# A new head for a one-core encoder step: first weights in five pieces among the input tiles, squares behind the parts, a split sum for the total, four plain pairs

## Chip, cores and metric

The kernel runs on one core of one Trainium2 chip. The metric is the device time of one execution in microseconds. Three runs of the kernel before gave a median of 1302.38 us (1302.33 to 1303.26).

## What is computed

One layer of a streaming encoder for 512 new frames and 64 frames of a running stream, together T = 576 columns with D = 1024 features, in f32:

```python
x = x + 0.5 * swiglu_ffn(rms_norm(x, ffn1_norm), ffn1_w_gate_up, ffn1_w_down)
h = rms_norm(x, mix_norm); p = h @ w_in
# two convolution branches and a gated merge through w_a_out, w_b_out, w_out
x = x + merged @ w_out
x = x + 0.5 * swiglu_ffn(rms_norm(x, ffn2_norm), ffn2_w_gate_up, ffn2_w_down)
y = rms_norm(x, final_norm)

def swiglu_ffn(x, w_gate_up, w_down):
    gate, up = jnp.split(x @ w_gate_up, 2, axis=-1)
    return (jax.nn.silu(gate) * up) @ w_down
```

The change concerns the head: the first norm and the first columns of the first FFN (DFF = 2816, in 22 columns of 128).

## The kernel before

**Layout and products.** Features lie on the 128 partitions, the 576 columns on the free axis; x is eight tiles `X[0..7]`. A product of f32 accuracy is made of f32r products: every weight and every activation is split into a high part (a cast on ACT) and a low part (value minus high part). One step k of one output tile (`mm`, lines 392 to 403) is six matmuls of 128 x 288: high·high, high·low and low·high, for both halves of the columns. A full tile over eight k has 48 matmuls.

**Norm.** The gain is put into the operands (`split_scaled`, line 484); the inverse root R is multiplied in after the product. `Sum` (line 492) adds the eight squares. `total` multiplies the sum by a matrix of ones: with `gather` called before (line 527) the sum has been split into two f32r operands, otherwise it runs in plain f32, which PE does in two passes per matmul. `rstd` (line 549) takes the root on ACT and refines it by three DVE instructions.

**Gate and up columns.** Columns i < `PLAIN[f]` are plain: a gate tile g_i and an up tile u_i, 96 matmuls. The others are pairs by a scheme with seven half products (`pair`, 84 matmuls) that needs derived operands of x: `Forms.scale` (two ACT instructions), `combine` (four DVE instructions and two casts), `split` (two low parts), each for four indices p; and sums of weights on DVE. Before, the first three columns are plain.

**Order.** Each engine runs its instructions in the order in which the program writes them (`Ordered`, line 68). Weights come through `Stream` (line 193): `load` issues raw tiles on SP's queue into six slots, `begin` casts the high part on ACT and, for units marked "dma", writes the negative, to which a DMA of POOL adds the raw value; `end` makes the low part on DVE for the others. `get` keeps the stream six units ahead, so a product also issues casts and low parts of later weights.

**PSUM** is one pool of four tiles (`mmps`, line 126), two banks each. A tile's slot is free when its last reader in program order is done: for the total that is the tensor_scalar of `rstd`, for a gate tile the multiplication by R in `gate` (line 707), for an up tile that in `hidden` (line 711).

**The head** (lines 605 to 674): FIRST are the tiles g0, u0 and g1, multiplied together step by step as k arrives. Their weights come as nine raw tiles (k = 1, 3 and 4 steps at a time, `FIRST_KS`), alternating with the x tiles on SP's queue; the gains are ACT's first transfer. POOL makes three of the squares and the last three low parts. Then four units are prepared (u1 and g2), `scale(0)`, `scale(1)` and `combine(0)` follow, the eight steps of FIRST are multiplied with the total (plain f32) before the last, and u1 is multiplied. Inside `ffn`, the columns are then gated in turn, with steps of `Forms` given in a list and put between (`forming`); `split(0)` and `split(1)` make their low parts by POOL's DMA.

Of the kernel before, what the change touches and what calls it, by code (L numbers as in the profile page):

```python
# [20 lines left out]
KU = KT // 2  # L21
# [10 lines left out]
R_CA = 4  # L32
# [11 lines left out]

HALVES = ((0, H), (H, T))
LATE_SPANS = (((0, 304),), ((304, T),))
FIRST_KS = (1, 3, 4)
WARM = 10


PLAIN = {"f1": 3, "f2": 1}

IN_TURN = (0, 4, 1, 5, 2, 6, 3, 7)

# [1 line left out]
SIX = ((0, 0), (1, 0), (0, 1), (1, 1), (2, 0), (2, 1))  # L56
# [47 lines left out]
def tile_encoder_step(  # L104
# [44 lines left out]
    def psum2():  # L149
        return mmps.tile([P, 2, 512], F32, tag="mm", name=nm("mm"))  # L150
# [16 lines left out]
    ones = cpool.tile([P, P], F32, tag="ones", name="ones")  # L167
# [3 lines left out]
    pool.memset(eps, EPS)  # L171
    prm_src = params.rearrange("p (r j) -> p r j", j=KT)
    gains = cpool.tile([P, R_CA, KT], F32, tag="gains", name="gains")
    sca.dma_start(gains, prm_src[:, :R_CA, :])
    prm = cpool.tile([P, NPAR - R_CA, KT], F32, tag="prm", name="prm")
    hst = cpool.tile([P, KT, NHIST], F32, tag="hst", name="hst")
    X = [cpool.tile([P, T], F32, tag=f"x{j}", name=f"x{j}") for j in range(KT)]
    def table(func):

        t = cpool.tile([P, 1], F32, tag="table", name=nm("table"))  # L180
        sca.activation(t, eps, func)

    sca.copy(ones_r, ones)

    warm = psum2()
    for _ in range(WARM):
# [6 lines left out]
    class Stream:  # L193
# [108 lines left out]
    ws = Stream(6)  # L302
    plan = {}
    homes = [0]

    def home(other):

        homes[0] += 1
        return ("u", other)[homes[0] % 2]

    def plan_tile(name, w, row0, ks, col0, other, home_of=None):
        plan[name] = []
        for k in ks:
            r = ws.raw(w, row0, k, col0)
            plan[name].append(ws.unit(r, k, home_of or home(other), "dma"))
            row0 += k * P

    FIRST = [("f1", "g", 0), ("f1", "u", 0), ("f1", "g", 1)]

    def gu_col(part, i):  # L320
        return i * P + (DFF if part == "u" else 0)
# [22 lines left out]
    def plan_ffn(f, gu, dn):  # L344
        for g, grp in enumerate(GROUPS):
            for i in grp:
                if i >= PLAIN[f]:
                    plan_pair(f, gu, i)
                    continue
                for part in "gu":  # L350
                    if (f, part, i) not in plan:
                        plan_tile((f, part, i), gu, 0, (KU, KU), gu_col(part, i), "g")
            n = len(grp)
            for j in range(KT):
                late = f == "f2" and grp[-1] == FT - 1 and j in LATE
                plan_tile(
                    (f, "d", g, j), dn, grp[0] * P, (n - n // 2, n // 2), j * P, "g",
                    "act" if late else None,
                )

    for name in FIRST:
        plan[name] = []
    row = 0
    for k in FIRST_KS:
        for name in FIRST:
            r = ws.raw(ffn1_gu, row, k, gu_col(*name[1:]))
            plan[name].append(ws.unit(r, k, "act", "dve"))
        row += k * P
    plan_ffn("f1", ffn1_gu, ffn1_dn)

    def plan_mixer(name, w, col):
# [17 lines left out]
    plan_ffn("f2", ffn2_gu, ffn2_dn)  # L389


    def mm(ps, w, kk, xs, first, last, spans=HALVES):


        (whi, wlo), (xh, xl) = w, xs
        parts = ((whi, xh), (whi, xl), (wlo, xh))
        for n, s in SIX:
            if s < len(spans):
                (a, b), (i, e) = parts[n], spans[s]
                pe.matmul(  # L400
                    ps[:, s, : e - i], a[:, kk, :], b[:, i:e],
                    start=first and n == 0, stop=last and n == 2,
                )
# [64 lines left out]
    def low(v, hi):  # L468
        lo = atile(F32R)
        dve.tensor_tensor(lo, v, hi.bitcast(F32), op=ALU.subtract)  # L470
        return lo

    def low_by_dma(v, hi):
        lo = atile(F32R)
        sca.mul(lo, hi.bitcast(F32), -1.0)
        pool.dma_start(lo.bitcast(F32), v, accum_op=ALU.add)
        return lo

    def split(v):

        hi = high(v)
        return hi, low(v, hi)
# [66 lines left out]
    def rstd(total, spans=HALVES):  # L549

        a, t = ttile(), ttile()
        r = rpool.tile([P, T], F32, tag="r", name=nm("r"), bufs=2)
        tot = total.total(spans)
        span = slice(spans[0][0], spans[-1][1])
        shaped = halves if len(spans) == 2 else (lambda v: v)
        a, t, y = a[:, span], t[:, span], r[:, span]
        dve.tensor_scalar(shaped(a), tot, 1.0 / D, EPS, op0=ALU.mult, op1=ALU.add)
        sca.activation(y, a, AF.Abs_reciprocal_sqrt)
        dve.scalar_tensor_tensor(t, y, -0.5, y, op0=ALU.mult, op1=ALU.mult)
        dve.tensor_tensor(t, t, a, op=ALU.mult)  # L560
        dve.scalar_tensor_tensor(y, t, 1.5, y, op0=ALU.add, op1=ALU.mult)
        return r


    class Forms:
# [19 lines left out]
                dve.tensor_tensor(out, a, b, op=op)  # L585
            self.t[p] = [(v, high(v)) for v in (c, d)]

        def split(self, p, by_dma=False):
            self.parts[p] = [
                (hi, (low_by_dma if by_dma else low)(v, hi)) for v, hi in self.t.pop(p)  # L590
            ]

        def operands(self, xg):

# [10 lines left out]
    ss = Sum()  # L605
    xg = []
    def load(j):
        nc.sync.dma_start(X[j], x[j * P : (j + 1) * P, :])

    def begin(j):  # L610
        xg.append(split_scaled(X[j], par(j, R_N1)))

    def weights(lo=dve):
        for _ in FIRST:
            ws.prep(lo)

    def squares(*js):
        for j in js:
            ss.square(X[j], pool if j in (0, 2, 4) else sca)

    load(0)
    begin(0)
    squares(0)
    weights()
    load(1)
    begin(1)
    weights()
    load(2)
    load(3)
    begin(2)  # L630
    begin(3)
    squares(1, 2)
    weights(pool)
    for j in range(4, KT):
        load(j)
    ss.add(dve)
    ss.add(dve)
    squares(3)
    begin(4)
    begin(5)  # L640
    ss.add(dve)
    squares(5, 4)
    ss.add(dve)
    ss.add(dve)
    begin(6)
    begin(7)
    squares(6, 7)
    ss.add(dve)
    ws.eager = True
    for _ in range(4):  # L650
        ws.prep()
    forms1 = Forms(R_N1)
    forms1.scale(0)
    forms1.scale(1)
    forms1.combine(0)
    nc.sync.dma_start(prm, prm_src[:, R_CA:, :])
    table(AF.Abs_reciprocal_sqrt)
    first = {name: psum2() for name in FIRST}
    firstw = {}
    for name in FIRST:  # L660
        firstw[name] = []
        for n in plan[name]:
            w = ws.ready.pop(n)
            firstw[name] += [(w, kk) for kk in range(ws.units[n][1])]
    for k in range(KT):
        if k == KT - 1:
            R1 = rstd(ss)
        for name in FIRST:
            w, kk = firstw[name][k]
            mm(first[name], w, kk, xg[k], k == 0, k == KT - 1)  # L670
    early.update(first)
    name = ("f1", "u", 1)
    ps = product(name, xg)
    early[name] = ps


    def split_early(p):
        one.split(p, by_dma=True)

    def update(j, ps, R=None):  # L680

# [137 lines left out]
    ffn(  # L819
        "f1", xg, ss, finish1, one, R1,  # L820
        (
            ((split_early, 0), (one.scale, 2), (one.combine, 1)),
            ((split_early, 1), (one.scale, 3), (one.combine, 2)),
            ((one.split, 2), (one.combine, 3)),
            ((one.split, 3),),
        ),
# [370 lines left out]
```

## Time and profile before

| | |
|---|---|
| Median of three runs | 1302.38 us |
| The profiled execution | 1303.07 us, its span 1301.3 us |
| PE busy (matmuls) | 1286.3 us, 9746 instructions |
| DVE, ACT, POOL busy | 892.0, 778.5, 400.5 us |
| HBM read | 113.81 MB |

The span is what the profile shows from the first to the last instruction of the core. Busy times of PE contain the modelled tail of pipelined matmuls, so back-to-back matmuls are better told from their start times. A bracket behind a line of the timeline tells how long the engine was idle before it and what ended that.

### The profile page before, as it was taken

To read this page: it belongs to the slowest core of one execution; us is meant where nothing else is said; L and a number is where in the kernel's file an instruction comes from. 1 tells how busy PE (TensorE), PEld (TensorE's weight loads), DVE (VectorE), ACT (ScalarE), POOL (GpSimd) and SP (SyncE) were. 2 spreads that over 40 slices of the span, in tenths; PEclk is the share of its full clock that TensorE was granted. 3 is DMA by queue.
4 is the path that set the end of the run, shared out by engine and by line. 5 is a ranking of instruction groups with operands and counts; after the bars stand their busy time and mean duration, and the time that the engine had idled before them with its cause. 6 is when DMAs were issued, how large, how long until landed. Compare 5 with 4: busy or idle time off the path is not lost.

```text
span 1301.3 us, 25714 instructions
## 1 busy us (share of the span) xinstructions
PE 1286.3 (99%) x9746; PEld 1282.5 (99%) x9746; DVE 892.0 (69%) x1460; ACT 778.5 (60%) x1374; POOL 400.5 (31%) x502
## 2 busy tenths in 40 slices
PE   9999999999999999999999999999999999999997
PEld 8999999999999999999999999999999999999996
DVE  6758758748945899888895260336967848847955
ACT  8755655645677655555554684457665655654664
POOL 4242332332242544322221322222142141241233
PEclk9999999999999999999999999999999999999999
DMA  9797787886798797877775978776687796796784
GB/s 245 141 189 160 148 185 157 165 192 147 152 195 182 167 216 173 175 166 170 172 168 125 199 158 178 154 166 142 138 169 165 162 192 149 163 206 136 161 178 107
DMA packets 290108, 218.40 MB, mean 168 GB/s; under 512 B 15680, under 2 KB 251200, under 8 KB 289984
## 3 DMA queue, kind: packets, MB, share of 16 engines
q0 software_dynamic: 60768, 100.30, 46.4%
q1 hardware_dynamic: 227488, 115.62, 31.4%
q8 instruction: 77, 1.26, 0.4%
q10 hardware_dynamic: 1728, 0.84, 0.2%
q14 instruction: 47, 0.39, 0.1%
HBM read 113.81 MB, written 2.62 MB: 89 GB/s over the span
## 4 chain that ended last, share of the span: by engine, by line
PE 90%; issue 4%; DMA 2%; ACT 1%; POOL 1%; DVE 1%; DVEq 0%; POOLq 0%; ACTq 0%; SPq 0%
PE mm L80 90%; DMA g<-raw 1%; DMA raw<-in_ffn_w_gate_up_dram 1%; POOL act L80 1%; DVE tmp L80 0%; ACT u L80 0%; DMA gains<-in_params_dram 0%; POOL g L80 0%; ACT tmp L80 0%; ACT g L80 0%; DVE acc L80 0%; ACT act L80 0%; DVE x L80 0%; DVE g L80 0%; POOL tmp L80 0%
## 5 line engine op out<-in xcount | busy, mean ns | idle before, releaser
L80 PE MATMUL mm<-act,u 128*128 128x288 f32 x4686 | 660.9, 294 | 0.7 <-DVE u L80 0.5
L80 PEld LDWEIGHTS mm<-act,u 128*128 128x128 f32 x4686 | 630.9, 188 | 1.2 <-DVE u L80 0.7
L80 PE MATMUL mm<-act,g 128*128 128x288 f32 x2766 | 398.6, 294 | 2.1 <-DMA g<-raw 2.0
L80 PEld LDWEIGHTS mm<-act,g 128*128 128x128 f32 x2766 | 376.5, 188 | 2.9 <-DMA g<-raw 2.8
L80 POOL DMA_DIRECT2D u<-raw x204 | 176.3, 864 | 550.4 <-ACT u L80 492.2
L80 PE MATMUL mm<-act,act 128*128 128x288 f32 (+2 forms) x2244 | 307.6, 293 | 1.4 <-DVE act L80 1.4
L80 PEld LDWEIGHTS mm<-act,act 128*128 128x128 f32 x2244 | 297.8, 188 | 2.4 <-DVE act L80 2.1
L80 POOL DMA_DIRECT2D g<-raw x124 | 108.6, 876 | 247.2 <-ACT g L80 188.2
L80 ACT CAST u<-raw 128x512 fp32r<-128x512 f32 (+2 forms) x204 | 117.1, 574 | 108.6 <-PE mm L80 76.5
L80 DVE SCALAR_TENSOR_TENSOR w<-g,prm,w 128x606 f32<-128x606 f32 x232 | 179.3, 844 | 1.4 <-ACT w L80 1.4
L80 DVE TENSOR_TENSOR tmp<-mm,tmp 128x288 f32<-128x288 f32 (+1 forms) x244 | 109.7, 458 | 72.9 <-PE mm L80 53.5
L80 ACT ACTIVATE u<-u 128x512 fp32r<-128x512 f32 (+2 forms) x204 | 121.1, 594 | 6.5
L80 POOL DMA_DIRECT2D act<-raw x90 | 78.9, 876 | 50.6 <-ACT act L80 49.5
L80 DVE SCALAR_TENSOR_TENSOR tmp<-mm,r 128x576 f32<-128x576 f32 x48 | 36.3, 757 | 78.0 <-PE mm L80 77.8
L80 ACT CAST g<-raw 128x512 fp32r<-128x512 f32 (+2 forms) x124 | 67.7, 546 | 35.3 <-DMA raw<-in_ffn_w_down_dram 14.7
L80 ACT CAST act<-tmp 128x576 fp32r<-128x576 f32 x84 | 56.2, 674 | 52.4 <-DVE tmp L80 51.6
L80 ACT CAST g<-w 128x512 fp32r<-128x512 f32 x80 | 49.6, 619 | 63.0 <-DVE w L80 56.6
L80 ACT CAST u<-w 128x512 fp32r<-128x512 f32 x80 | 49.5, 619 | 61.9 <-DVE w L80 55.7
L80 DVE TENSOR_TENSOR act<-tmp,act 128x576 fp32r<-128x576 f32 x80 | 59.3, 754 | 21.3 <-ACT act L80 19.8
L80 ACT ACTIVATE g<-g 128x512 fp32r<-128x512 f32 (+2 forms) x124 | 70.4, 568 | 3.9
L80 ACT CAST act<-raw 128x512 fp32r<-128x512 f32 (+2 forms) x99 | 57.6, 583 | 16.1 <-PE mm L80 11.0
L80 DVE TENSOR_TENSOR w<-raw,raw 128x512 f32<-128x512 f32 x80 | 54.8, 685 | 11.0 <-DMA raw<-in_ffn_w_gate_up_dram 11.0
(88 smaller groups left out, 814.1 us busy)
## 6 DMA issues: line engine op xcount, KB each, us to landing
raw<-in_ffn_w_gate_up_dram SPq DMA_DIRECT2D x173, 256.0 KB, 3.4
u<-raw POOLq DMA_DIRECT2D x145, 256.0 KB, 4.0
raw<-in_w_in_dram SPq DMA_DIRECT2D x112, 256.0 KB, 3.4
act<-raw POOLq DMA_DIRECT2D x80, 256.0 KB, 4.8
raw<-in_ffn_w_down_dram SPq DMA_DIRECT2D x96, 192.0 KB, 3.5
g<-raw POOLq DMA_DIRECT2D x65, 256.0 KB, 3.8
g<-raw POOLq DMA_DIRECT2D x43, 192.0 KB, 4.5
u<-raw POOLq DMA_DIRECT2D x43, 192.0 KB, 4.5
```

The lines of the kernel that those rows point to most:

```text
L80: return self.tc.keep_in_program_order(fn(*args, **kwargs))
```

## The change

`PLAIN["f1"]` goes from 3 to 4, `FIRST` is u0, g0, g1, and the weights of FIRST no longer pass through the stream. They come in five pieces of 1, 1, 2, 2 and 2 steps k, each of a transfer for u0 and one for g0 and g1 together, among the x tiles on SP's queue; x0 and the gains go out on ACT's queue. Piece 0 is split by DVE alone, the others by ACT (high) and DVE (low). All squares are on ACT, each behind the parts that PE needs next; the sum is gathered and totalled in f32r, behind the last step of FIRST. The low parts of u1, g2 and u2 are made on DVE (`low="dve"`), as are the derived operands of p = 0 and 1. `scale(1)` and the preparation of g2 stand behind `combine(0)`.

```diff
-FIRST_KS = (1, 3, 4)
+FIRST_KS = (1, 1, 2, 2, 2)
-PLAIN = {"f1": 3, "f2": 1}
+PLAIN = {"f1": 4, "f2": 1}
-    sca.dma_start(gains, prm_src[:, :R_CA, :])
...
-    sca.copy(ones_r, ones)
...
-    FIRST = [("f1", "g", 0), ("f1", "u", 0), ("f1", "g", 1)]
+    FIRST = [("f1", "u", 0), ("f1", "g", 0), ("f1", "g", 1)]
...
-                        plan_tile((f, part, i), gu, 0, (KU, KU), gu_col(part, i), "g")
+                        plan_tile(
+                            (f, part, i), gu, 0, (KU, KU), gu_col(part, i), "g",
+                            low="dve" if f == "f1" and i < 3 else "dma",
+                        )
...
     def load(j):
-        nc.sync.dma_start(X[j], x[j * P : (j + 1) * P, :])
+        (sca if j == 0 else nc.sync).dma_start(X[j], x[j * P : (j + 1) * P, :])
+    pieces = []
+    def load_piece(k):
+        row = P * sum(n for n, _, _ in pieces)
+        raws = []
+        for col, cols in ((gu_col("u", 0), P), (gu_col("g", 0), 2 * P)):
+            if len(pieces) < 3:
+                t = wraw.tile([P, KU * P], F32, tag="raw", name=nm("raw"))[:, : k * cols]
+            else:
+                t = gtile(n=k * cols)
...
+            nc.sync.dma_start(t, ffn1_gu[0, row : row + k * P, col : col + cols].rearrange(
+                "(k p) n -> p k n", p=P))
+            raws.append(t)
+        pieces.append((k, raws, []))
+    def split_piece(n, by):
+        k, raws, parts = pieces[n]
+        for raw in raws:
...
+            if by is dve:
+                dve.tensor_copy(hi, raw)
+            else:
+                by.copy(hi, raw)
+            dve.tensor_tensor(lo, raw, hi.bitcast(F32), op=ALU.subtract)
+            parts.append((hi, lo))
...
+    first = {name: psum2() for name in FIRST}
+    def multiply(k):
+        n, kk = piece_of(k)
+        up, gates = pieces[n][2]
+        for six in (SIX,) if k > 0 else (((0, 0), (2, 0), (0, 1), (2, 1)), ((1, 0), (1, 1))):
+            for name, (hi, lo), c in zip(FIRST, (up, gates, gates), (0, 0, P)):
+                w = hi[:, :, c : c + P], lo[:, :, c : c + P]
+                mm(first[name], w, kk, xg[k], k == 0, k == KT - 1, six=six)
     load(0)
+    sca.dma_start(gains, prm_src[:, :R_CA, :])
+    sca.copy(ones_r, ones)
+    load_piece(FIRST_KS[0])
+    load(1)
+    load_piece(FIRST_KS[1])
+    load(2)
+    load_piece(FIRST_KS[2])
+    load(3)
+    load(4)
+    load_piece(FIRST_KS[3])
+    load(5)
+    load(6)
+    load_piece(FIRST_KS[4])
+    load(7)
+    split_piece(0, dve)
     begin(0)
     begin(1)
+    split_piece(1, sca)
+    multiply(0)
     begin(2)
+    split_piece(2, sca)
+    multiply(1)
+    ss.square(X[0])
     begin(3)
+    ss.square(X[1])
+    multiply(2)
...
+    begin(7)
+    ss.add(dve)
+    for j in (5, 6, 7):
+        ss.square(X[j])
+    multiply(6)
     ss.add(dve)
     ss.add(dve)
     ws.eager = True
-    for _ in range(4):
-        ws.prep()
+    ws.prep()
+    ss.gather()
+    ws.prep()
     forms1 = Forms(R_N1)
     forms1.scale(0)
+    table(AF.Abs_reciprocal_sqrt)
+    multiply(7)
+    R1 = rstd(ss)
+    table(AF.Silu)
+    forms1.combine(0)
+    ws.prep()
+    ws.prep()
     forms1.scale(1)
-    forms1.combine(0)
     nc.sync.dma_start(prm, prm_src[:, R_CA:, :])
...
-    for k in range(KT):
-        if k == KT - 1:
-            R1 = rstd(ss)
-        for name in FIRST:
-            w, kk = firstw[name][k]
-            mm(first[name], w, kk, xg[k], k == 0, k == KT - 1)
     early.update(first)
     name = ("f1", "u", 1)
     ps = product(name, xg)
     early[name] = ps
...
-            ((split_early, 0), (one.scale, 2), (one.combine, 1)),
-            ((split_early, 1), (one.scale, 3), (one.combine, 2)),
+            ((one.split, 0), (one.combine, 1)),
+            ((one.scale, 2),),
+            ((one.split, 1), (one.combine, 2)),
+            ((one.scale, 3),),
             ((one.split, 2), (one.combine, 3)),
             ((one.split, 3),),
```

## Rows read from the trace of the kernel before

**Rows 1.** The page's first part: busy time of each engine, its share of the span and its instructions.

```profile
PE 1286.3 (99%) x9746; PEld 1282.5 (99%) x9746; DVE 892.0 (69%) x1460; ACT 778.5 (60%) x1374; POOL 400.5 (31%) x502
```

**Rows 2.** The windows view, two stretches of the span: length, busy us (and instructions) of PE, PEld (weight load), DVE, ACT and POOL, granted TensorE clock, DMA share, GB/s. A pipelined matmul counts as busy to its modelled end.

```profile
5.29:75.36 70.07, 65.93 (x476) 63.64 (x476) 52.92 (x87) 56.78 (x98) 26.22 (x27) 1.00 0.85 188
75.36:1280.00 1204.64, 1204.49 (x9171) 1204.26 (x9171) 826.41 (x1351) 712.37 (x1257) 366.38 (x465) 1.00 0.79 168
```

**Rows 3.** The timeline of PE up to 80 us: start, length, operation, out<-in, shapes, count, and in brackets the idle time before it with what ended it. `act`, `g` and `u` are the tiles that hold the weights' parts; `acc` and `tmp` with `ones` are the total of squares.

```profile
5.29 5.69 PE L80 MATMUL mm<-act,act 128*128 128x288 f32 x37
11.60 9.97 PE L80 MATMUL mm<-act,act 128*128 128x288 f32 x72 [0.62 <-DVE act L80]
22.39 2.52 PE L80 MATMUL mm<-act,act 128*128 128x288 f32 x17 [0.82 <-DVE act L80]
24.75 0.65 PE L80 MATMUL mm<-acc,ones 128*128 128x288 f32 x2
...
26.48 2.75 PE L80 MATMUL mm<-act,act 128*128 128x288 f32 x18
29.06 3.32 PE L80 MATMUL mm<-act,g 128*128 128x288 f32 x24
32.22 3.32 PE L80 MATMUL mm<-act,u 128*128 128x288 f32 x24
35.38 3.32 PE L80 MATMUL mm<-act,g 128*128 128x288 f32 x24
...
48.02 1.74 PE L80 MATMUL mm<-act,g 128*128 128x288 f32 x12
...
57.47 1.59 PE L80 MATMUL mm<-act,u 128*128 128x288 f32 x10 [0.48 <-DVE u L80]
...
60.84 1.60 PE L80 MATMUL mm<-act,g 128*128 128x288 f32 x10 [1.51 <-DMA g<-raw]
62.28 1.75 PE L80 MATMUL mm<-act,u 128*128 128x288 f32 x12
...
73.41 1.48 PE L80 MATMUL mm<-act,g 128*128 128x288 f32 x10
75.36 3.71 PE L80 MATMUL mm<-act,g 128*128 128x288 f32 x26 [0.47 <-DMA g<-raw]
```

**Rows 4.** The start: from the timeline the warm-up on PE and ACT's first high part; then from the DMA view the issue of x0 (at 0.74), x1 (at 2.60) and x7 (at 9.73): queue, count, KB each, us from issue to landing.

```profile
1.00 4.64 PE L80 MATMUL mm<-ones 128*128 128x128 f32 x20 [1.00 <-POOL eps L80]
4.01 0.78 ACT L80 ACTIVATE act<-x,gains 128x576 fp32r<-128x576 f32 x1 [1.24 <-DMA gains<-in_params_dram]
x<-in_x_dram SPq DMA_DIRECT2D x1, 288.0 KB, 3.1
x<-in_x_dram SPq DMA_DIRECT2D x1, 288.0 KB, 3.7
x<-in_x_dram SPq DMA_DIRECT2D x1, 288.0 KB, 6.5
```

**Rows 5.** The timeline of DVE, one line from the stretch in which POOL computes (two low parts).

```profile
15.11 3.15 DVE L80 SCALAR_TENSOR_TENSOR act<-x,gains,act 128x576 fp32r<-128x576 f32 x2 [0.39 <-ACT act L80]
```

**Rows 6.** The timeline of DVE and ACT behind the total of squares (`r` is the inverse root, `tmp<-mm,r` gate 0, the 128x288 instructions a combine, `u<-w,u` and `w<-raw,raw` work on weights), then lines of ACT: two casts of weights, two of activations, two of scale.

```profile
26.89 0.76 DVE L80 TENSOR_SCALAR tmp<-mm 128x576 f32<-128x576 f32 x1 [0.83 <-PE mm L80]
28.72 0.67 ACT L80 ACTIVATE r<-tmp 128x576 f32<-128x576 f32 x1
29.43 0.76 DVE L80 SCALAR_TENSOR_TENSOR tmp<-r 128x576 f32<-128x576 f32 x1 [1.78 <-ACT r L80]
30.22 0.76 DVE L80 TENSOR_TENSOR tmp<-tmp,tmp 128x576 f32<-128x576 f32 x1
33.02 0.75 DVE L80 TENSOR_TENSOR tmp<-mm,r 128x576 f32<-128x576 f32 x1
33.68 0.45 DVE L80 TENSOR_TENSOR tmp<-w 128x288 f32<-128x288 f32 x1
...
34.91 0.45 DVE L80 TENSOR_TENSOR tmp<-w,tmp 128x288 f32<-128x288 f32 x1
42.71 0.69 DVE L80 TENSOR_TENSOR u<-w,u 128x512 fp32r<-128x512 f32 x1
43.31 0.69 DVE L80 TENSOR_TENSOR w<-raw,raw 128x512 f32<-128x512 f32 x1
11.80 1.16 ACT L80 CAST act<-raw 128x512 fp32r<-128x512 f32 x2
26.07 1.23 ACT L80 CAST act<-tmp 128x576 fp32r<-128x576 f32 x2
36.81 1.43 ACT L80 ACTIVATE w<-x,gains 128x576 f32<-128x576 f32 x2
```

**Rows 7.** The page's DMA issues: POOL's accumulating transfers that make a weight's low part; count, KB each, median us to landing.

```profile
u<-raw POOLq DMA_DIRECT2D x145, 256.0 KB, 4.0
```

**Rows 8.** The windows view of the tail, columns as in rows 2; behind the last column of counts the granted clock.

```profile
1292.00:1293.00 1.00, 0.34 (x2) 0.00 (x0) 0.44 (x1) 0.15 (x1) 0.00 (x0) 1.00 0.23 78
1295.00:1296.00 1.00, 0.00 (x0) 0.00 (x0) 1.00 (x2) 0.00 (x0) 0.00 (x0) 1.00 0.00 0
1296.00:1297.00 1.00, 0.00 (x0) 0.00 (x0) 1.00 (x3) 0.00 (x0) 0.00 (x0) 0.74 0.57 183
1297.00:1298.00 1.00, 0.00 (x0) 0.00 (x0) 0.37 (x1) 0.00 (x0) 0.00 (x0) 0.50 1.00 336
```

More of the change, by code (lines that the diff above doesn't have):

```diff
@@ L309, in home, with plan_tile @@
         return ("u", other)[homes[0] % 2]
-    def plan_tile(name, w, row0, ks, col0, other, home_of=None):
+    def plan_tile(name, w, row0, ks, col0, other, home_of=None, low="dma"):
         plan[name] = []
@@ L314, in plan_tile @@
             r = ws.raw(w, row0, k, col0)
-            plan[name].append(ws.unit(r, k, home_of or home(other), "dma"))
+            plan[name].append(ws.unit(r, k, home_of or home(other), low))
             row0 += k * P
-    FIRST = [("f1", "g", 0), ("f1", "u", 0), ("f1", "g", 1)]
+    FIRST = [("f1", "u", 0), ("f1", "g", 0), ("f1", "g", 1)]
     def gu_col(part, i):
@@ L362, in tile_encoder_step @@
         plan[name] = []
-    row = 0
-    for k in FIRST_KS:
-        for name in FIRST:
-            r = ws.raw(ffn1_gu, row, k, gu_col(*name[1:]))
-            plan[name].append(ws.unit(r, k, "act", "dve"))
-        row += k * P
     plan_ffn("f1", ffn1_gu, ffn1_dn)
@@ L389, in tile_encoder_step, with mm @@
     plan_ffn("f2", ffn2_gu, ffn2_dn)
-    def mm(ps, w, kk, xs, first, last, spans=HALVES):
+    def mm(ps, w, kk, xs, first, last, spans=HALVES, six=SIX):
         (whi, wlo), (xh, xl) = w, xs
         parts = ((whi, xh), (whi, xl), (wlo, xh))
-        for n, s in SIX:
+        for n, s in six:
             if s < len(spans):
@@ L470, in low @@
         dve.tensor_tensor(lo, v, hi.bitcast(F32), op=ALU.subtract)
[L471 to L476, printed above, removed]
         return lo
@@ L586, in combine, with split @@
             self.t[p] = [(v, high(v)) for v in (c, d)]
[L588 to L591, printed above, removed]
+        def split(self, p):
+            self.parts[p] = [(hi, low(v, hi)) for v, hi in self.t.pop(p)]
         def operands(self, xg):
@@ L607, in load @@
     def load(j):
-        nc.sync.dma_start(X[j], x[j * P : (j + 1) * P, :])
+        (sca if j == 0 else nc.sync).dma_start(X[j], x[j * P : (j + 1) * P, :])
[8 more added lines that the diff above has]
+                t = gtile(n=k * cols)
+            t = t.rearrange("p (k n) -> p k n", n=cols)
+            nc.sync.dma_start(t, ffn1_gu[0, row : row + k * P, col : col + cols].rearrange(
+                "(k p) n -> p k n", p=P))
+            raws.append(t)
+        pieces.append((k, raws, []))
@@ L610, in begin @@
+    def split_piece(n, by):
+        k, raws, parts = pieces[n]
+        for raw in raws:
+            cols = raw.shape[2]
+            hi, lo = (
+                atile(F32R, k * cols).rearrange("p (k n) -> p k n", n=cols) for _ in range(2)
+            )
+            if by is dve:
[4 more added lines that the diff above has]
+            parts.append((hi, lo))
     def begin(j):
@@ L611, in begin, with piece_of @@
         xg.append(split_scaled(X[j], par(j, R_N1)))
[L613 to L619, printed above, removed]
-    load(0)
+    def piece_of(k):
+        for n, size in enumerate(FIRST_KS):
+            if k < size:
+                return n, k
+            k -= size
+    first = {name: psum2() for name in FIRST}
[6 more added lines that the diff above has]
+                mm(first[name], w, kk, xg[k], k == 0, k == KT - 1, six=six)
@@ L622, in tile_encoder_step @@
+    load(0)
+    sca.dma_start(gains, prm_src[:, :R_CA, :])
[13 more added lines that the diff above has]
+    split_piece(0, dve)
     begin(0)
-    squares(0)
-    weights()
-    load(1)
     begin(1)
-    weights()
-    load(2)
-    load(3)
+    split_piece(1, sca)
+    multiply(0)
@@ L630, in tile_encoder_step @@
     begin(2)
+    split_piece(2, sca)
+    multiply(1)
+    ss.square(X[0])
     begin(3)
[L632 to L635, printed above, removed]
+    ss.square(X[1])
+    multiply(2)
+    begin(4)
+    ss.add(dve)
+    split_piece(3, sca)
+    ss.square(X[2])
+    multiply(3)
+    begin(5)
+    ss.add(dve)
+    ss.square(X[3])
+    multiply(4)
+    begin(6)
+    ss.add(dve)
+    split_piece(4, sca)
+    ss.square(X[4])
+    multiply(5)
+    begin(7)
+    ss.add(dve)
@@ L636, in tile_encoder_step @@
+    for j in (5, 6, 7):
+        ss.square(X[j])
+    multiply(6)
     ss.add(dve)
     ss.add(dve)
[L638 to L648, printed above, removed]
     ws.eager = True
-    for _ in range(4):
-        ws.prep()
+    ws.prep()
+    ss.gather()
+    ws.prep()
     forms1 = Forms(R_N1)
     forms1.scale(0)
+    table(AF.Abs_reciprocal_sqrt)
+    multiply(7)
+    R1 = rstd(ss)
@@ L654, in tile_encoder_step @@
+    table(AF.Silu)
+    forms1.combine(0)
+    ws.prep()
+    ws.prep()
     forms1.scale(1)
-    forms1.combine(0)
     nc.sync.dma_start(prm, prm_src[:, R_CA:, :])
[L657 to L664, printed above, removed]
-    for k in range(KT):
-        if k == KT - 1:
-            R1 = rstd(ss)
-        for name in FIRST:
-            w, kk = firstw[name][k]
-            mm(first[name], w, kk, xg[k], k == 0, k == KT - 1)
@@ L674, in tile_encoder_step @@
     early[name] = ps
-    def split_early(p):
-        one.split(p, by_dma=True)
     def update(j, ps, R=None):
```

## The prediction

> **What bounds the kernel now.** The page's busy shares come first: TensorE (PE) is busy for 1286.3 of 1301.3 us, DVE for 69% and ACT for 60% [rows 1]. The windows say where the other 15 us lie: from 75.36 us to 1280 PE is busy for 1204.49 of 1204.64 us, while before 75.36 some 4 us are missing, although PE counts as busy in a pipelined matmul's tail [rows 2]. So I read PE's own timeline up to 75.36, where its last stall of the head ends [rows 3]. After that point only the count of matmuls sets the time, and this change alters none there: pairs 4 to 21 and all later stages stay as they are. The forecast therefore is one number: when does PE reach the same point, ten products into the first down projection?
>
> A product in full flow costs 3.16/24 = 0.1317 us: 24 from 29.06 to 32.22 and again to 35.38 [rows 3]. Before the point stand 144 products of the first three tiles (37 + 72 + 17, then 18 behind the total), 144 of u1, g2 and u2, 84 each for pairs 3 and 4, and ten: 466, or 61.37 us. The total of squares in plain f32 takes 24.75 to 26.48 = 1.73. From 5.29 to 75.36 are 70.07 us, so 6.97 are waits: in the first 126 products 19.46 - 16.59 = 2.87, in the 18 behind the total 2.58 - 2.37 = 0.21, in pair 3 (48.02 to 62.28) 14.26 - 11.06 = 3.20, in pair 4 0.07, in the ten 1.95 - 1.32 = 0.63 [rows 3]. The waits in pair 3 are for DVE's low parts and for lows that a DMA adds (57.47, 60.84).
>
> **The change part by part.** *Four plain pairs.* Pair 3 becomes two plain tiles of 48 products for one pair of 84: 12 more, +1.58 us. It buys time for the derived operands.
>
> *The total* now is four f32r passes of 0.1317 = 0.53 instead of 1.73: -1.20. The gather that makes this possible adds two DVE instructions and a cast; by my ledger its low part is there 1.6 us before PE needs it.
>
> *The start.* Before, PE's ten warm-up products (20 passes) last to about 5.3, and the first high part is ready at 4.01 + 0.78 = 4.79 [rows 4], so warm-up ended last. Now x0 goes out on ACT's queue, the gains behind it at about 1.2, and two weight pieces and x1 leave on SP's queue at once. Lower bound: x0 lands after 3.1 us as before and the gains do not wait, start 5.3. Upper bound: the gains take the 6.5 us of a transfer issued into a full queue, landing 7.7, start 8.5 [rows 4]. The nearest row is x1, issued at 2.60 with the first x and three small weights before it: 3.7 us. So gains issued at 1.2 land at about 4.9, the high part follows at 5.7, and PE starts at 5.75: +0.46. The Trainium skill ("DMA: Bandwidth & Descriptors", section "Issuing engines are not separate DMA queues") says that transfers of several issuing engines interleave on the same 16 DMA engines; had each queue its own, the lower bound would hold and the sum would be 0.46 lower. Before has no such pair of queues to show it.
>
> *The stretch of the first three tiles.* The bytes are the same and come in the order of use. Up to the last tile's parts ACT has eight high parts and five squares, at 0.78 at most (4.01), and eight casts at 0.58 at most (two in 1.16 at 11.80): 14.8 us, against 16.6 of PE before k = 7. DVE has eight low parts at 0.76 (29.43), four adds at 0.75 and twelve weight parts at 0.69 at most (42.71), most of them half as wide: under 17.4, by their widths about 14 [rows 4, 6]. In before DVE's instructions were stretched where POOL computed (two low parts in 3.15 us) [rows 5]; POOL computes nothing there now. By my ledger (each engine in program order, durations of the rows) PE's operands are ready 1 us early at k = 1, 1.5 at k = 2 and over 3 from k = 4. So here I put 0 waits and 0.3 for slow first products: the first 37 took 5.69 us instead of 4.87, part of it waits [rows 3]. Bounds: 0 to 2.87, as before.
>
> So the three tiles end at 5.75 + 0.3 + 18.96 = 25.0 and the total's last pass ends at T = 25.0 + 3 x 0.1317 + 0.29 = 25.7.
>
> *A new wait at u1.* PSUM holds four tiles of the pool. Three keep u0, g0 and g1, the fourth the total, and u1 can only have that one. Before, 18 products of k = 7 stood between the total and u1 and hid DVE's tensor_scalar of 0.76 (26.89) [rows 6]. Now they stand ahead of the total. PE waits from its last issue until T + 0.82 and needs 0.1 to refill: +1.08. Bounds: 0 if another slot were free, 1.2.
>
> *A new wait at g2.* Its slot is g0's, which gate 0 reads. Before, gate 0 ends at 33.77 and g2 starts at 35.38: 1.6 us to spare [rows 3, 6]. Now more stands ahead of it on DVE. From T: tensor_scalar to +0.79, ACT's root to +1.49, three Newton steps with the third starting at +3.11, combine(0) from +3.78 (four instructions, the last ending at +5.46: 33.68 to 34.91 and 0.45). ACT's second high part waits for that and starts at +5.49; behind it in ACT's order are the two casts of g2 (0.54 each, 11.80), scale(1) (0.67 each, 36.81) and the casts of u2, so u2's first cast runs from 5.49 + 0.57 + 1.08 + 1.34 = +8.48 to +9.09 (0.57 from 26.07: two in 1.23). Then DVE: u2's two low parts at 0.60 (42.71 to 43.31) and gate 0, from +10.33 to +11.08 [rows 6]. PE has finished u1 at T + 0.92 + 48 x 0.1317 = T + 7.24, so it waits 3.9 and refills 0.1: +3.97. Behind gate 0 on DVE stand split(0), combine(1) and the gate's product; behind g2 all of PE. Lower bound, DVE never waiting for ACT: 4 lows and gate 0 directly behind combine(0) end at +8.6, a wait of 1.4. Upper: one more ACT cast and its negative in between, 5.1. I take 3.97, as every wait in it follows from program order and a row.
>
> *Behind g2.* The ledger, with these waits in it, finds no further one: pair 4's operands of split(3) are ready at about 56 for a need at 63.5, gates 1 to 3 free their slots over 6 us early, and the last low of pair 4's weights, issued by POOL at about 65 and 4 us on its way, lands at 69 for a need at 71.6 [rows 7]. So pair 3's 3.20, pair 4's 0.07 and the 0.63 of the ten go. If g2's wait were absent, that cover would be gone too: the weight's low would land with under half a us to spare.
>
> **Sum:** 5.75 + 0.3 + 478 x 0.1317 (62.95) + 0.53 + 1.08 + 3.97 = 74.58, against 75.36: -0.78. The profiled execution took 1303.07 us (span 1301.3), 0.69 above the median 1302.38; I take the difference off both: 1302.3 profiled, 1301.6 as the median.
>
> **The rivals.**
> *A: g2 does not wait for gate 0* (a slot comes free earlier, or ACT does its casts ahead). For it: PE stood still nowhere for PSUM in before. Against it: four slots, and a gate that program order puts behind u2's lows. Then 3.97 goes and some 0.4 comes back at the down projection's first lows: 1301.6 - 3.6 = 1298.0.
> *B: slower, TensorE's clock falls in the pause at g2.* Place: the idle 3.9 us at about 33. In the tail PE's last pass lies in 1292 to 1293; the granted clock still is 1.00 in 1295 to 1296, 0.74 in the next us, then 0.50 (from 2.4 to 1.2 GHz) [rows 8]. So a pause only a little longer was enough there. Price: at the start PE works from 1.00, and the first products after 5.29 are still slow [rows 3, 4]: a stretch of some 5 us, half of which would be lost, 2.5. 1301.6 + 2.5 = 1304.1. It decides if the pause lasts longer than forecast. The Trainium skill ("TensorE: Matmul & The Clock Gate", section "Why this matters for your kernels") tells of pauses between bursts that bring the engine back to the lower level; the fall to 0.50 in the tail agrees, no pause in mid-kernel of before shows it, and where it holds 1304.1 is the time.
> *C: slower, the head starves.* The gains or early pieces land late: start at 7.1 instead of 5.75 and 1 us of waits at k = 1 and 2: 1301.6 + 2.4 = 1304.0; at the upper bounds 1306. For it: ten transfers share the queues in the first 5 us. Against it: the bytes of each k were there earlier than PE needs them.
> *D: the plain pair without the rest helps* (pair 3's stalls move to pair 4): 3.3 back, 1304.9. The ledger leaves 2 us of slack, which speaks against it.
>
> **How the numbers follow.** Forecast 0.60, A 0.16, B 0.08, C 0.12, D 0.04. The forecast's own range is 1300.0 to 1303.2, from the start's and chain's bounds that are near. To leave out no more than 2 in 10, half of A and most of B and C come in: 1298.3 to 1304.4. What a measurement of this kernel can tell from no change is 0.2%, 2.6 us: faster means under 1299.8, slower over 1305.0. Faster: A and a tail of the forecast (a chain 2 us shorter), 0.20. Slower: the upper parts of C, B and D, 0.09. The same: 0.71.
>
> **What would show it.** Right: PE's first real product near 5.75; no idle time between 7 and 25; a pause of about 1 us released by DVE's tensor_scalar, then 24 + 24 products and one of about 4 us before g2 that ends just behind DVE's `tmp<-mm,r`; nothing after that up to the down projection, which begins near 73.3. Wrong: no pause at g2, a granted clock below 1.00 near 35, waits for x or raw transfers before 20, or waits inside pair 4.

## The result, and the profile after

The changed kernel takes 1305.04 us (median of 21 runs, 1303.68 to 1310.66), the kernel before, beside it, 1303.44 (21 runs, 1302.21 to 1304.18): a ratio of 1.0015, 95% interval 1.0008 to 1.0022. The forecast was a little faster, it is a little slower. The profiled execution of after took 1305.16 us. The times below are medians of the fast executions: three far longer ones (1817.17 and 6843.95 us in experiment 6, and 2576.52 in experiment 8, whose median with it is 1298.52) are left out. The page of after answers to [rows 1]:

```profile
span 1303.4 us, 25701 instructions
...
PE 1287.0 (99%) x9754; PEld 1284.8 (99%) x9754; DVE 890.4 (68%) x1463; ACT 771.5 (59%) x1365; POOL 388.7 (30%) x487
```

The page says almost nothing: PE is busy for 99% before and after. The windows do, cut where the prediction cuts, at the first product and ten products into the first down projection:

```profile
5.64:77.02 71.38, 65.97 (x482) 65.53 (x483) 51.14 (x87) 52.10 (x91) 11.22 (x13) 0.95 0.62 152
77.02:1282.00 1204.98, 1204.98 (x9171) 1204.70 (x9170) 825.86 (x1351) 710.34 (x1255) 370.68 (x465) 1.00 0.80 167
```

Against [rows 2], the long part is the same (1204.98 with 9171 matmuls, where it was 1204.64), so the difference is in the head, as expected: the point lies at 77.02 (ten products, 1.32, behind the 75.70 shown below) instead of 75.36. These 1.66 us are most of the 2.09 between the two profiled executions (0.34 more lie in the long part) and agree with the 1.60 between the medians. But the column of the granted clock, 1.00 in [rows 2], reads 0.95. PE's timeline of the head, columns as in [rows 3]:

```profile
...
5.64 19.26 PE L81 MATMUL mm<-act,act 128*128 128x288 f32 x144 [0.56 <-ACT act L81]
24.74 0.69 PE L81 MATMUL mm<-tmp,ones_r 128*128 128x288 f32 x4
26.28 3.49 PE L81 MATMUL mm<-act,g 128*128 128x288 f32 x24 [0.85 <-DVE tmp L81]
29.60 3.39 PE L81 MATMUL mm<-act,u 128*128 128x288 f32 x24
37.55 5.36 PE L81 MATMUL mm<-act,g 128*128 128x288 f32 x24 [4.56 <-DVE tmp L81]
42.75 3.28 PE L81 MATMUL mm<-act,u 128*128 128x288 f32 x24
...
61.47 3.28 PE L81 MATMUL mm<-act,u 128*128 128x288 f32 x24
64.59 1.74 PE L81 MATMUL mm<-act,g 128*128 128x288 f32 x12
...
75.70 4.91 PE L81 MATMUL mm<-act,u 128*128 128x288 f32 x36
```

The 144 products of the first three tiles run in one line from 5.64 to 24.74, where [rows 3] has breaks of 0.62 and 0.82 and the total in between. Then two pauses: one at u1 (26.28) and one before g2 (37.55), both ended by a `tmp` of DVE. Behind them no bracket is left up to the down projection. One line doesn't fit: the first 24 products of g2 last from 37.55 to 42.75, 5.20 us, where 24 products usually take 3.16. The granted clock tells why (windows of one us, the clock is the third figure from the right):

```profile
34.00:35.00 1.00, 0.00 (x0) 0.00 (x0) 0.37 (x1) 1.00 (x3) 0.00 (x0) 1.00 0.06 16
35.00:36.00 1.00, 0.00 (x0) 0.00 (x0) 0.56 (x1) 1.00 (x3) 0.00 (x0) 0.53 0.74 219
...
40.00:41.00 1.00, 1.00 (x6) 1.00 (x5) 1.00 (x2) 0.94 (x2) 0.00 (x0) 0.50 0.98 170
41.00:42.00 1.00, 1.00 (x7) 1.00 (x6) 0.26 (x2) 1.00 (x3) 0.00 (x0) 0.56 1.04 178
42.00:43.00 1.00, 1.00 (x9) 1.00 (x9) 1.00 (x2) 1.00 (x3) 0.00 (x0) 1.00 0.17 31
```

PE stopped in the us before 33, the clock fell from 1.00 to 0.50 (2.4 to 1.2 GHz) early in 35 to 36, in the middle of the pause, and came back in 41 to 42, after PE had been multiplying since 37.55 at the lower level: six matmuls lie wholly or in part in 40 to 41, nine in 42 to 43.

Who ends the pause is seen on DVE and ACT behind the total; the lines answer to [rows 6]:

```profile
19.36 2.48 DVE L81 TENSOR_TENSOR acc<-acc,tmp 128x576 f32<-128x576 f32 x3
23.20 0.67 ACT L81 CAST tmp<-acc 128x576 fp32r<-128x576 f32 x1 [3.05 <-DVE acc L81]
23.91 0.76 DVE L81 TENSOR_TENSOR tmp<-acc,tmp 128x576 fp32r<-128x576 f32 x1 [0.79 <-ACT tmp L81]
24.30 1.44 ACT L81 ACTIVATE w<-x,gains 128x576 f32<-128x576 f32 x2
25.47 0.76 DVE L81 TENSOR_SCALAR tmp<-mm 128x576 f32<-128x576 f32 x1 [0.20 <-PE mm L81]
25.76 1.28 ACT L81 ACT_TABLE_LOAD   x1
27.16 0.67 ACT L81 ACTIVATE r<-tmp 128x576 f32<-128x576 f32 x1
33.07 0.69 DVE L81 TENSOR_TENSOR g<-raw,g 128x512 fp32r<-128x512 f32 x1 [1.26 <-ACT g L81]
36.05 0.69 DVE L81 TENSOR_TENSOR u<-raw,u 128x512 fp32r<-128x512 f32 x1
36.65 0.75 DVE L81 TENSOR_TENSOR tmp<-mm,r 128x576 f32<-128x576 f32 x1
```

Gate 0 (36.65) is queued behind u2's low part (36.05), and g2's first product follows 0.15 us after its end. But the root `r` began at 27.16, though its operand was there at 25.47 + 0.76 = 26.23: ACT was loading the table, late because the sum's high part came late (23.20, after an idle time of 3.05).

### The profile page after: what moved, and what is told of

Same layout as the page of the kernel before. It is cut to its first block, busy times and chain, and to the rows that moved or that the text cites. A ratio compares the mean times of both kernels' runs of the same rounds, so it can differ in the third digit from the quotient of the medians.

```text
span 1303.4 us, 25701 instructions
## 1 busy us (share of the span) xinstructions
PE 1287.0 (99%) x9754; PEld 1284.8 (99%) x9754; DVE 890.4 (68%) x1463; ACT 771.5 (59%) x1365; POOL 388.7 (30%) x487
## 4 chain that ended last, share of the span: by engine, by line
PE 96%; DVE 2%; ACT 1%; DMA 1%; issue 0%; DVEq 0%; SPq 0%; ACTq 0%
PE mm L81 96%; DVE acc L81 0%; DVE tmp L81 0%; DMA raw<-in_ffn_w_gate_up_dram 0%; ACT tmp L81 0%; ACT act L81 0%; DMA x<-in_x_dram 0%; DVE act L81 0%; ACT w L81 0%; DVE g L81 0%; DVE x L81 0%; ACT L81 0%; DVEq L1228 0%; DVE r L81 0%; ACT u L81 0%
## 5 line engine op out<-in xcount | busy, mean ns | idle before, releaser
L81 DVE TENSOR_TENSOR act<-tmp,act 128x576 fp32r<-128x576 f32 x84 | 62.2, 755 | 19.3 <-ACT act L81 17.9
L81 ACT CAST act<-raw 128x512 fp32r<-128x512 f32 (+3 forms) x94 | 55.6, 592 | 10.7 <-PE mm L81 7.5
```

Source lines behind the costliest of these rows:

```text
L81: return self.tc.keep_in_program_order(fn(*args, **kwargs))
```

## The experiments

Two theories of the slow 5.20 and of the pauses, to be told apart: the *slot theory* (u1 and g2 wait for a slot of PSUM, whose last reader stands far back in DVE's order) and the *clock theory* (the pause itself makes the next products slow). Rivals: PE waits for weights or operands, and the slow products are due to contention, since DMAs are busy there too (1.04 of 16 engines in 41 to 42). Each ratio below is to the kernel before, run on the same chip, with its 95% interval.

**1. The pause filled with work that nothing needs.**

```diff
+        if name == ("f1", "u", 1):
+            for _ in range(20):
+                pe.matmul(ps[:, 0, 320 : 320 + P], ones, ones, start=True, stop=True)
```

> The kernel after with 20 extra matmuls (ones by ones, 128 columns, results unused, into columns of u1's PSUM tile that nothing reads) behind u1, so that PE works through most of the pause of 4.85 us before g2. The pause itself is not shortened. Clock theory: the granted clock stays at 1.00 between 33 and 45, g2's first 24 products take about 3.2 us instead of 5.2, and the time falls by about 2.0 us against the kernel after, to a median near 1303.0. Rival (the slow products come from late operands or from transfers that run at the same time): the products stay at 0.24 us each and the time stays at about 1305.

Measured 1303.46 us, ratio 0.9997 (0.9988 to 1.0006). Two lines of PE's timeline and a window:

```profile
33.12 4.63 PE L82 MATMUL mm<-ones 128*128 128x128 f32 x40
37.70 3.46 PE L82 MATMUL mm<-act,g 128*128 128x288 f32 x24
...
39.00:40.00 1.00, 1.00 (x10) 1.00 (x9) 0.96 (x3) 0.23 (x2) 0.61 (x1) 1.00 1.18 265
```

g2 begins no earlier (37.70), but the clock stays at 1.00 and the 24 products take 41.00 - 37.70 = 3.30. The DMA share is as high as in after (1.18), so contention isn't the cause. Idle time of PE is: the same wait without the fall of the clock is 1.6 us cheaper between the medians (2.3 by the two ratios).

**2. Gate 0 right behind the root**, so that g0's slot comes free early.

```diff
     table(AF.Silu)
+    gate0()
     forms1.combine(0)
```

> The kernel after with gate 0 (g0 times R, then Silu) moved to directly behind the root, ahead of combine(0), the preparation of g2 and u2's low parts. Slot theory: g0's PSUM slot is free at about 31, before u1 ends at 32.8, so PE waits only for g2's weights, whose first low part is then about 0.7 us later than now (34.4): a pause of 1.0 to 1.8 us instead of 4.85, no fall of the clock; median 1305.0 - 3.0 to 3.8 - 2.0 = 1299.2 to 1300.0, less what then waits at pair 4 or the first down projection (up to 1 us more). Rival (the wait is for ACT's casts of g2's weights, as the weight loads' own releaser says): g2 still starts near 37.5 or later and the time stays at 1305.

Measured 1301.06 us, ratio 0.9981 (0.9972 to 0.9990):

```profile
33.87 3.63 PE L81 MATMUL mm<-act,g 128*128 128x288 f32 x24 [0.31 <-ACT g L81]
...
41.27 3.46 PE L81 MATMUL mm<-act,g 128*128 128x288 f32 x24 [0.62 <-ACT act L81]
```

DVE's line of hidden 0 (gate 0 times u0):

```profile
40.38 0.75 DVE L81 TENSOR_TENSOR tmp<-mm,tmp 128x576 f32<-128x576 f32 x1
```

g2 no longer waits for `tmp`, only 0.31 us for its own weights' high part, and the clock does not fall. The slot theory holds. Some of the gain expected is missing (1299.2 to 1300.0, less up to 1 us): PE now idles 0.62 us before the next tile, u2, for u0's slot, which hidden 0 frees at 41.13. The bracket names ACT, but u2 starts 0.14 behind hidden 0's end, as g2 started 0.15 behind gate 0 in after. In this execution 24 products also take 3.23 us from u2 to pair 3, a cost with no known cause (last section).

**3. Three plain columns again**, all else as after.

```diff
-PLAIN = {"f1": 4, "f2": 1}
+PLAIN = {"f1": 3, "f2": 1}
```

> The kernel after with three plain columns in the first FFN, the new head unchanged. Buying-time theory: 12 products fewer, -1.58 us, but pair 3 now begins at about 55 where its derived operands of p = 3 are ready only near 58 to 59 and its weights' low parts later still, so waits of 3 to 6 us come back inside pair 3: median 1306.5 to 1309.5. Rival (the fourth plain column only costs its 12 products, the pause at g2 has already given the time): 1303.4.

Measured 1309.55 us, ratio 1.0043 (1.0031 to 1.0056). A line of DVE, two of PE and a window:

```profile
37.17 0.69 DVE L81 TENSOR_TENSOR w<-w,raw 128x512 f32<-128x512 f32 x1 [2.00 <-DMA raw<-in_ffn_w_gate_up_dram]
...
39.88 5.34 PE L81 MATMUL mm<-act,g 128*128 128x288 f32 x24 [6.70 <-DVE tmp L81]
...
60.16 0.54 PE L81 MATMUL mm<-act,u 128*128 128x288 f32 x2 [2.46 <-DVE act L81]
...
62.00:63.00 1.00, 1.00 (x6) 1.00 (x5) 0.99 (x2) 0.26 (x1) 0.15 (x1) 0.50 1.02 166
```

Twelve products fewer, and 4.5 us longer: the wait before g2 grows to 6.70, a second one of 2.46 stands in pair 3, and behind it the clock falls a second time. Pair 3's 84 products take 70.01 - 54.53 = 15.48 instead of 11.06: 4.42 us, the waits that were expected, with the fall of the clock in them. About 2 us more come at g2, where nothing was expected: DVE's sums of pair 3's weights, due sooner now, wait 2.00 us for a raw transfer and stand ahead of gate 0. The fourth plain column buys time, as the prediction said, for the weights too and not only for the derived operands.

**4. Experiment 2 with g2's preparation ahead of `combine(0)`.**

```diff
     gate0()
+    ws.prep()
+    ws.prep()
     forms1.combine(0)
-    ws.prep()
-    ws.prep()
     forms1.scale(1)
```

> As the early gate 0, and g2's two weight units prepared ahead of combine(0), right behind gate 0. Slot theory with nothing else in the way: g2's parts are there at about 32, PE goes on from u1 to g2 without a pause; then the lag of DVE and ACT shows at pair 4 or at the first lows of the down projection, 0 to 2 us. Against the kernel after -4.85 - 2.04 + 0 to 2: median 1298.2 to 1300.2. Rival (weights or another reader hold g2 as before): no better than 1304.

Measured 1304.07 us, ratio 1.0006 (0.9997 to 1.0015): a miss. PE's timeline, DVE's (hidden 0) and a window:

```profile
32.82 3.32 PE L81 MATMUL mm<-act,g 128*128 128x288 f32 x24
...
42.95 4.94 PE L81 MATMUL mm<-act,g 128*128 128x288 f32 x24 [3.64 <-ACT act L81]
```

```profile
42.05 0.75 DVE L81 TENSOR_TENSOR tmp<-mm,tmp 128x576 f32<-128x576 f32 x1
```

```profile
44.00:45.00 1.00, 1.00 (x6) 1.00 (x5) 1.00 (x3) 1.00 (x3) 0.00 (x0) 0.50 0.65 107
```

g2 starts at 32.82 without any pause, and 42.95 - 32.82 - 6.32 = 3.81 of the 4.95 us reappear one tile later: u2 needs u0's slot, which hidden 0 frees at 42.80. The clock falls there too, from 43.15 on. The slot given earlier moved the wait to the next slot in the ring, and the new order made that one later: hidden 0 starts at 42.05 instead of 40.38 in experiment 2, because `combine(0)` and all behind it now follow g2's low parts.

**5. The table load ahead of the gather** (the 0.9 us by which gate 0 was later than forecast).

```diff
     ws.prep()
+    table(AF.Abs_reciprocal_sqrt)
     ss.gather()
...
-    table(AF.Abs_reciprocal_sqrt)
     multiply(7)
```

> The kernel after with one instruction pair moved: the table load for the inverse root stands ahead of the gather on ACT, where ACT is idle for 3 us, instead of behind scale(0). Theory of the mis-sized step: in the kernel after the root waited for this load (25.76 to 27.05) and not for its operand (ready at 26.22), which made gate 0 and with it g2 0.9 us late. Then the root starts near 26.3, the pause at g2 is about 4.0 instead of 4.85 us, and the time falls by 0.9 to about 1304.1; if the shorter pause leaves the clock at 1.00, by 2.9 to about 1302.1. Rival (another wait in the chain takes over): pause and time unchanged, 1305.

Measured 1304.83 us, ratio 1.0011 (1.0002 to 1.0019).

```profile
36.68 6.10 PE L81 MATMUL mm<-act,g 128*128 128x288 f32 x24 [3.77 <-DVE tmp L81]
...
39.00:40.00 1.00, 1.00 (x6) 1.00 (x6) 1.00 (x3) 0.93 (x2) 0.00 (x0) 0.50 1.06 174
```

The root now begins at 26.28 and g2 at 36.68, 0.87 earlier, as expected. But its 24 products take 42.57 - 36.68 = 5.89, since more of them lie in the stretch at 0.50, which lasts until 42.66: of 0.87 us about 0.2 is left between the medians, less than their intervals can tell from nothing.

**6. The total in plain f32 ahead of k = 7, as before**, with its `gather` left out.

```diff
-    ss.gather()
...
-    multiply(7)
     R1 = rstd(ss)
+    multiply(7)
     table(AF.Silu)
```

> The kernel after with the total as it was in the kernel before: not split, in plain f32, ahead of the products of k = 7; all else new. It costs about 1.2 us more on PE for the passes, but 18 products hide the tensor_scalar again (u1's pause of 1.1 us goes), and the root starts about 1.5 to 2.2 us earlier, so that gate 0 ends near 35.3 and g2's pause is 2.3 to 2.9 us. Theory (the order of the total makes both pauses long): median 1302.8 if the clock still falls, 1300.8 if it does not. Rival (the split sum itself is what gains, the pauses don't depend on it): no faster than 1305, up to 1306.

Measured 1302.91 us, ratio 0.9994 (0.9985 to 1.0003).

```profile
24.62 2.74 PE L81 MATMUL mm<-act,act 128*128 128x288 f32 x18
27.20 3.32 PE L81 MATMUL mm<-act,g 128*128 128x288 f32 x24
...
36.23 4.74 PE L81 MATMUL mm<-act,g 128*128 128x288 f32 x24 [2.55 <-DVE tmp L81]
```

The 18 products of k = 7 hide the tensor_scalar again, and u1 (27.20) has no pause. The costlier total (22.82 to 24.62, 1.80) is repaid: the root starts sooner (25.83), the pause before g2 shrinks to 36.23 - 27.20 - 6.32 = 2.71 us, and the low clock lasts from 35.78 to 39.19 only. Without the gather the table load is early too (22.87), so some 0.9 of the 1.33 us that the root gains is what experiment 5 gained.

**7. Experiment 2 with hidden 0 in the head too**, behind `combine(0)`; g2's casts ahead of it, its low parts behind.

```diff
     gate0()
+    for _ in range(2):
+        ws.add()
+        ws.begin()
     forms1.combine(0)
+    hidden0()
+    ws.end()
+    ws.end()
-    ws.prep()
-    ws.prep()
     forms1.scale(1)
```

> As the early gate 0, and also the product of the gate with u0 in the head (it frees u0's slot), behind combine(0); g2's casts ahead of combine(0), its low parts behind. Slot theory: the early gate 0 alone leaves PE two pauses, 0.3 to 0.55 us for g2's cast and 0.6 to 0.8 us for u0's slot at u2; both go and only u1's pause of 1.1 us is left: about 1.3 us less than the early gate 0 alone, median near 1299.7 (1299.2 to 1300.5). Rival (what PE gains here it gives back at pair 4 or the down projection): 1301.

Measured 1299.16 us, ratio 0.9966 (0.9953 to 0.9978), as expected:

```profile
34.32 2.91 PE L81 MATMUL mm<-act,g 128*128 128x288 f32 x20 [0.43 <-DVE g L81]
```

Both slots come free in time, and the clock never falls. What is left at g2 is a wait of 0.43 us for its own low parts, four products into the tile. The profiled execution, 1301.46 us, is the slowest of the five; it also has waits of 0.28 in pair 4 and 0.40 in the down projection.

**8. Experiments 5 and 7 together.**

> As f3_hidden0, with the table load ahead of the gather too. If no pause behind u1's is left, the 0.9 us that the chain gains hides nothing more and the time is that of f3_hidden0 within 0.4; if f3_hidden0 still has a pause at g2 or u2, up to 0.9 less. Median 1298.9 to 1299.9.

Measured 1298.20 us, ratio 0.9961 (0.9948 to 0.9974): faster than both kernels, and 0.7 us below the range expected. The wait at g2 of experiment 7 is the condition under which up to 0.9 less was expected.

```profile
26.34 3.49 PE L81 MATMUL mm<-act,g 128*128 128x288 f32 x24 [0.85 <-DVE tmp L81]
29.67 3.39 PE L81 MATMUL mm<-act,u 128*128 128x288 f32 x24
32.89 3.39 PE L81 MATMUL mm<-act,g 128*128 128x288 f32 x24
...
69.83 4.91 PE L81 MATMUL mm<-act,u 128*128 128x288 f32 x36
```

Only u1's pause is left; the down projection begins at 69.83 instead of 75.70.

**9. Experiment 8 with the gains ahead of x0 on ACT's queue.**

```diff
+    sca.dma_start(gains, prm_src[:, :R_CA, :])
     load(0)
-    sca.dma_start(gains, prm_src[:, :R_CA, :])
```

> f4_table_too with the gains ahead of x0 on ACT's queue; nothing else. It asks what the start term of the prediction hangs on. In f4_table_too x0 was issued at 0.74 and the gains at 1.19; ACT's first high part begins at 4.71 us, behind the gains. If the order of issue on ACT's queue decides, the gains now land near 4.2 and x0 near 4.5, the first high part begins at about 4.5, PE's first product at 5.3 instead of 5.54, and the rest of the head moves up by the same: 1298.3, against 1298.52. Rival: the landings are set by the bytes of both queues together, then x0, the larger one, lands as late as the gains did and the start stays at 5.5: 1298.5. Either way no new wait and a granted clock of 1.00 throughout the head.

Measured 1298.40 us, ratio 0.9964 (0.9951 to 0.9978). The timeline of ACT, and the DMA view of the start:

```profile
5.09 1.53 ACT L81 ACTIVATE act<-x,gains 128x576 fp32r<-128x576 f32 x2 [1.83 <-DMA x<-in_x_dram]
```

```profile
x<-in_x_dram ACTq DMA_DIRECT2D x1, 288.0 KB, 3.8
...
gains<-in_params_dram ACTq DMA_DIRECT2D x1, 16.0 KB, 2.2
```

The gains land 2.2 us after their issue (3.4 in experiment 8), x0 after 3.8 (3.2). The first high part comes 0.38 later than in experiment 8, and PE's first product at 5.92 instead of 5.54, where 5.3 or 5.5 was expected: a miss for both theories. The time is the same within its spread. The order on one queue shifts which of the two is late, and nothing is won. What the 0.38 us costs isn't shown, since the plain columns ran at 3.16 us per 24 products here and at 3.23 in experiment 8's trace.

**10. Experiment 8 with the total beside u0 and g0**, in columns of their PSUM tiles that nothing uses, so that u1 finds a free slot; g2's parts ahead of `combine(0)`.

```diff
-    R1 = rstd(ss)
+    R1 = rstd_beside(ss)
...
+        for s, out in enumerate((up[:, 0], up[:, 1], gate[:, 0])):
+            for m, (one, v) in enumerate(total.terms):
+                pe.matmul(out[:, H : H + n], one, v[:, s * n : (s + 1) * n],
+                          start=m == 0, stop=m == 1)
```

> f4_table_too with the total of squares written into unused PSUM columns beside u0 and g0 (six passes of 192 columns, two tensor_scalar instructions), so that u1 finds the pool's fourth slot free; g2's casts and low parts go ahead of combine(0), since PE asks for them about 1 us earlier. Slot theory of the wait at u1: its pause of 1.1 us (idle 1.08, ended by tensor_scalar) goes; u1 begins right behind the total near 25.4 us, g2 near 31.8 with at most 0.3 of waits, u2 near 38.2 behind hidden 0: 1297.4 to 1297.8. Bounds: a pass of 192 columns is not in any trace; at the price per column of 288 the six cost 0.53 us as the four did, at that of plain f32 (1.73 us for 1152 columns before) they cost about 1.7 and half of the gain is gone: 1298.5. Rival (u1 waits for the engine's reading of the total, not for the slot): u1 still begins at 26.3, 1298.5.

Measured 1298.18 us, ratio 0.9960 (0.9948 to 0.9973).

```profile
25.19 0.81 PE L81 MATMUL mm<-tmp,ones_r 128*128 128x192 f32 x6
25.84 3.35 PE L81 MATMUL mm<-act,g 128*128 128x288 f32 x24
...
32.18 3.32 PE L81 MATMUL mm<-act,g 128*128 128x288 f32 x24
...
67.77 1.60 PE L81 MATMUL mm<-act,g 128*128 128x288 f32 x10 [0.36 <-DMA g<-raw]
...
70.93 3.65 PE L81 MATMUL mm<-act,u 128*128 128x288 f32 x26 [0.24 <-DMA u<-raw]
```

u1's pause is gone (25.84, right behind the total), so it was the slot. But of the 0.9 us saved there (0.65 from the total's start to u1, where after has 1.54) nothing is left between the medians, 1298.18 and 1298.20, and 1297.4 to 1297.8 was expected: pair 4 and the down projection now wait for low parts that a DMA adds, as the prediction had it of a head without pauses.

## Why the prediction was wrong, point by point

*The place.* Right: only the head changed, and the two new waits are where they were put, with the releasers that were named (tensor_scalar at u1, gate 0 behind u2's low parts at g2; experiments 2, 6 and 10 show it). What the plain column and the new order were costed at holds too: no wait in the first 144 products, none in pair 4 and up to the point.

*The sum.* The point was put at 74.58 and lies at 77.02, 2.44 later. By its terms: the start is 5.64 (forecast 5.75): -0.11. The first three tiles take 19.10 (19.26): -0.16. From there the total and u1's pause take 26.28 - 24.74 = 1.54 (0.53 + 1.08): -0.07. The pause before g2 is, over 48 products at 0.1317, 37.55 - 26.28 - 6.32 = 4.95 (3.97): +0.98. The remaining 286 products take 77.02 - 37.55 = 39.47 instead of 37.67: +1.80. The level was off too: the forecast stands on a median of 1302.38 from three runs, and beside the change the kernel before took 1303.44. Of the 3.44 us between 1301.6 and 1305.04 this is 1.06; the other 2.38 agree with the 2.44.

*First failed step: the size of the wait at g2.* The prediction had the root at T + 0.79 (it came at 27.16 - 25.43 = T + 1.73), and the gather's low part ready "1.6 us before PE needs it". It was ready at 23.91 + 0.76 = 24.67, 0.07 before the total began at 24.74. With the gather late, scale(0) and the table load, which stand behind it in ACT's order, were late too, and the root began at 27.16 instead of 26.23. About 0.2 us of the gather's lateness is the three adds on `acc`, each of which needs the one before: they start 0.86 apart (0.76 + 2 x 0.86 = 2.48), where the ledger had 0.75. Why the rest came 1.5 us later than in the ledger stays open; DVE shows no idle time from 13.29 to the last add's end at 23.11. What failed in the chain is plain: it goes from tensor_scalar straight to the root and has no term for the table load (1.28 us) in between. Experiment 5 moves that load alone and g2 starts 0.87 earlier.

*Second failed step, and the larger: the pause was priced at its own length.* Rival B, the fall of the clock, had its place (about 33), its sign and nearly its price (2.5; measured 5.20 - 3.16 = 2.04 in g2's first 24 products, of which 0.24 comes back, as later products take 3.12 per 24), but the chance of 0.08 and the condition were wrong: "it decides if the pause lasts longer than forecast". The clock also fell in experiment 5, whose pause of 36.68 - 26.30 - 6.32 = 4.06 us is nearly the forecast's, and in experiment 6 with 2.71. That B's total, 2.5 over the forecast, comes so near the 2.44 is luck: 1.80 of it are the clock, and 0.64 the other terms, which B left as they were. The two mechanisms aren't alternatives: whoever forecast the pause had to forecast the fall. The tail [rows 8], where the clock was still 1.00 some 3 us after PE's last pass, was read as a bound, though it was one instance: in after the clock fell at 35.06, 2.1 us after PE's last product ended (29.60 + 3.39 = 32.99). The Trainium skill ("TensorE: Matmul & The Clock Gate", section "Why this matters for your kernels"), which says that an idle gap between bursts of matmuls brings the lower level back and which the prediction set beside that row, is borne out in mid-kernel: the granted clock fell to 0.50 in the pause before g2, and it stayed at 1.00 when experiment 1 filled that pause.

*Rival A* had about the right size for a head without that wait: 4.4 us under the kernel before, where experiments 8 and 10 lie 5.2 under theirs (that 1298.0 itself agrees with 1298.20 and 1298.18 is luck: the larger gain and the higher level cancel), and the waits it foresaw at the down projection's first low parts are those of experiment 10. But the change as made leaves g2 behind gate 0. *C* did not happen, nor *D*.

## What to carry to other kernels

A pause of PE costs its length and, once the clock has fallen, about half of the time from PE's return until the clock is back (2.04 of 4.33 us in after, 37.55 to 41.88); so a pause that is forecast must be charged with both, and a shorter one may gain almost nothing (experiment 5) while one filled with products that nothing needs does (experiment 1). Where PSUM slots go round, list for each new tile the slot it takes and everything that stands ahead of the slot's last reader on its engine; freeing one alone moves a part of the wait to the next (0.62 us in experiment 2, 3.81 in experiment 4), freeing both was worth 6.8 us here, the table load's move included (experiment 8 against after). And the place of a table load in ACT's order counts like that of any instruction: put it where ACT has nothing that others wait for.

## What was not expected of the hardware

The clock stayed at 1.00 in the short pauses (1.51 idle at 60.84 in before, [rows 3]; 0.85 at u1; those of experiments 2 and 10) and fell in all the longer ones (2.46, 2.55, 3.64, 3.77, 4.56 and 6.70 idle, in experiments 3, 6, 4, 5, after and 3); no run has one between 1.51 and 2.46. In experiment 4 it fell at 43.15, after PE had already begun again at 42.95. How long it stays low differs: 6.8 us in after, 3.4 in experiment 6.

Two things stay open. The runs of after spread from 1303.7 to 1306.2 (without one of 1310.66), and those with a mean granted clock of 0.997 are mostly the shorter, those with 0.994 the longer; that the low stretch has different lengths from run to run would explain it, but only one of these runs has a trace. And 24 products at a granted clock of 1.00 took 3.23 us in the plain columns of experiments 1, 2 and 8, 3.16 in before and, from u2 on, in the other experiments, and 3.12 in after behind its pause (42.75 to 61.47 in six steps): some 2 to 3% for which no row names a cause.
